# A recurrent layer's output products one unit later, its transposes, scores and second split later

## The chip, the cores and the metric

The kernel runs on one core of a Trainium2 chip. The metric is the device time of one execution in microseconds (us), here the median of three runs. The core has five engines that work from queues of their own: TensorE (PE in the rows; its weight loads are PEld), VectorE (DVE), ScalarE (ACT), GpSimd (POOL) and SyncE (SP), which only issues loads here. DMA transfers are issued by SP and by GpSimd.

## What is computed

Two layers of width 2048 on 256 positions. Layer 0 is a gated mixture with pooling, layer 1 the recurrent layer that the change touches; each is followed by a normalisation, a convolutional feed-forward block and another normalisation. The recurrent layer, cut to what matters:

```python
h = x @ od_w_in[o]                               # 2048 -> 4 x 2048
q, f_logit, inp, g = jnp.split(h, 4, axis=-1)
f = lb + (1.0 - lb) * sigmoid(f_logit)           # 16 heads of 128, chunks of 64 positions
qh, kh, vh = heads(silu(q)), heads(1.0 - f), heads(inp)
bcum = cumsum(heads(log(f)), axis=3)
q_dec, k_dec = qh * exp(bcum), kh * exp(-bcum)
att = where(mask, q_dec @ k_dec.T, 0.0)          # scores
o = att @ vh + q_dec @ state                     # state: decayed sum of k_end.T @ vh
y = rms_norm(o, od_norm_g) * sigmoid(g)          # outputs
mix = y @ od_w_out[o]                            # "down" products
```

## The kernel before

Every product is computed in three parts (high times high, high times low, low times high half of a float32 number), so each weight block of 512 x 512 is loaded from memory as 1 MB and copied twice: ScalarE rounds it to `wh` (line 178), VectorE writes the rest `wl` (line 181). Blocks are used in one fixed list of "feeds". `take` (line 192) hands out the next one, after it has issued the copies of the block two places ahead; three pairs of copies fit. Plain blocks (tag "w") have three raw buffers, loaded by SP as soon as the copy that frees a buffer has been issued and has run.

In the recurrent layer the 16 heads are worked in four head groups `hg`. A head group has two *units*: u0 gives the gates f and g, u1 gives q and the input v. A unit (`strassen`, line 399) multiplies two 1024-row parts by seven products P1 to P7 instead of eight, and the other 1024 rows plainly, as four blocks "s". A product P is 12 matmuls (128 x 128 by 128 x 512), a block "s" 24. P3, P5, P6 and P7 use combinations of the activations (`sh` in the rows), P1, P2, P4 and "s" the activations themselves (`xh`). The weights of P7, P6, P4 come from one raw buffer `a` (tag "qa"), those of P3 and P5 from `b` ("qb"). `a` is loaded by SP when P4 of the unit before has been copied; then GpSimd adds another block onto it by an accumulating load (line 110), which waits until the first load has landed; this sum is P7's operand. After P7's copy another block is accumulated (P6's operand), after P6's copy `b` becomes a - b on VectorE (line 113, P5's operand) and a third block is accumulated onto `a` (P4's operand).

Between the products of a unit stand "o" entries: `down` (line 577), the product of the finished output of an earlier head group with one of four column blocks of `od_w_out`, 2 x 12 matmuls, each half followed by a sum into the residual on VectorE (lines 572 and 574). How many downs a unit has chooses its order from `UNIT_R` (0, 1 or 2 downs). Before the change u0 of group hg has two downs of group hg - 1 and u1 the other two; in group 3 each unit has one, and two follow the units.

The small steps of a head group (gates `pb`, `pe`, `pk`; queries `pq`; scores `pa`, `px`; state `pu`; outputs `po`; transposes of the output `pt`) are put in by due times: `later(n, fn)` (line 314) asks for a step, `tick` (line 317) counts down, and 24 matmuls count as 1. So the order of issue is written by hand through the unit's order and these numbers; the build may still put an instruction ahead of one that it takes not to be ready. Each engine then runs its queue in that order.

Of the kernel before, what the change touches and what calls it, by code (L numbers as in the profile page):

```python
# [10 lines left out]
F32R = mybir.dt.float32r  # L11
# [7 lines left out]
P = 128  # L19
# [8 lines left out]
UNIT_R = (("P1", "P7", "s", "P3", "s", "P6", "P2", "P5", "s", "P4", "s"),  # L28
          ("P1", "s", "P7", "s", "P3", "P2", "P6", "o", "P5", "s", "P4", "s"),
          ("P1", "s", "P7", "s", "P3", "P2", "P6", "o", "P5", "o", "P4", "s", "s"))  # L30
UNIT = ("P1", "s", "P2", "s", "P3", "o", "P7", "o", "P6", "o", "P5", "o", "P4", "s", "s")
BUFS = 3
EDGE = 244
# [2 lines left out]
class Weights:  # L36
# [61 lines left out]
                if ap is not None:  # L98
                    self.std([ap])

    def chain(self, aps, rest, others=()):


        nc = self.nc
        a, b = self._load(aps[3], "qa"), self._load(aps[2], "qb")
        unit = UNIT_R[len(others)]
        rest, others = iter(rest), iter(others)

        def add(ap):
            nc.gpsimd.dma_start(a["tile"].rearrange("p k n -> p (k n)"), ap, accum_op=ALU.add)  # L110

        def t1():
            nc.vector.tensor_tensor(out=b["tile"], in0=a["tile"], in1=b["tile"], op=ALU.subtract)
            add(aps[1])

        a["then"] = lambda: add(aps[2])
        products = {"P7": (a, (), None, lambda: add(aps[0])), "P3": (b,), "P6": (a, (b,), None, t1),
                    "P5": (b,), "P4": (a,)}
        plain = {"P1": aps[0], "P2": aps[1]}
        for f in unit:  # L120
            if f in products:
                self._feed(*products[f])
            else:
                ap = plain[f] if f in plain else next(rest if f == "s" else others, None)
                if ap is not None:
                    self.std([ap])
# [76 lines left out]
def block_kernel(ctx: ExitStack, tc: tile.TileContext, a, out):  # L203
# [42 lines left out]
    W.phase += 1  # L246
    wi, wo = a["w_od_in"], a["w_od_out"]
    for hg in range(4):
        n_out = 2 if hg < 3 else 1
        for u, (c1, c2) in enumerate(((4 + hg, 12 + hg), (hg, 8 + hg))):  # L250
            if hg == 0 and u == 0:
                W.std([wi[c, g] for c in (c1, c2) for g in range(4)])
            else:
                outs = [wo[c, hg - 1] for c in range(u * n_out, (u + 1) * n_out)] if hg else []
                W.chain([wi[c1, 0], wi[c1, 1], wi[c2, 1], wi[c2, 0]],
                        [wi[c1, 2], wi[c1, 3], wi[c2, 2], wi[c2, 3]], outs)
    W.std([wo[c, 2] for c in (2, 3)])
    W.std([wo[c, 3] for c in range(4)])
    plan_ffn(1)
# [15 lines left out]
    def split(dst, src, hs, scale=None):  # L275

        h, l = dst[0][hs], dst[1][hs]
        if scale is None:
            A.activation(h, src, AF.Copy)
            V.tensor_tensor(out=l, in0=src, in1=h.bitcast(F32), op=ALU.subtract)  # L280
        else:
            A.activation(h, src, AF.Copy, scale=scale)
            V.scalar_tensor_tensor(out=l, in0=src, scalar=scale, in1=h.bitcast(F32),
                                   op0=ALU.mult, op1=ALU.subtract)
# [29 lines left out]
    def later(n, fn):  # L314
        waiting.append([n, fn])
# [513 lines left out]
    with ExitStack() as pools:  # L829
# [31 lines left out]
        def heads4(hg):  # L861
# [13 lines left out]
            def after_f(t, ps, f):  # L875
                kh = wk.tile([P, 512], F32, name="kh", tag="tb", bufs=2)
                A.activation(f, ps, AF.Sigmoid)
                V.tensor_tensor(out=f, in0=f, in1=rows["omlb"], op=ALU.mult)
                V.tensor_tensor(out=f, in0=f, in1=rows["lb"], op=ALU.add)
                if t == 1:  # L880
                    rows["ng"] = row("ng", a["norm_g"][qs].rearrange("(o n) -> o n", o=1))
                V.tensor_scalar(out=kh, in0=f, scalar1=-1.0, scalar2=1.0, op0=ALU.mult, op1=ALU.add)
                A.activation(f, f, AF.Ln)
                fh = wk.tile([P, 512], F32R, name="fh", tag="fh", bufs=1)
                fl = wk.tile([P, 512], F32R, name="fl", tag="fl", bufs=1)
                split((fh, fl), f, np.s_[:, :])
                later(1.5 + t, lambda: gates(t, fh, fl, kh))

            def gates(t, fh, fl, kh):

# [30 lines left out]
            def queries(t, q):  # L921
                pq = aux.tile([P, 4, P], F32, name="pq", tag="aux")
                for k in range(4):
                    transpose(pq[:, k], q[:, heads[k]])
                if t == 1:
                    dec = small.tile([P, 4, 1], F32, name="dec")
                    V.tensor_copy(dec, eb[1][:, :, 63:64])
                qd[t] = eb[t]
                V.tensor_tensor(out=qd[t], in0=pq, in1=eb[t], op=ALU.mult)
                if t == 1:  # L930

                    qx[1] = wk.tile([P, 4, P], F32, name="qx", tag="fh", bufs=1)
                    V.tensor_copy(qx[1][:, :, lo], qd[1][:, :, lo])
                    for k in range(4):
                        V.tensor_scalar(out=qx[1][:, k, hi], in0=qd[1][:, k, hi], scalar1=dec[:, k],
                                        scalar2=None, op0=ALU.mult)
                later(1, lambda: scores(t))

            def scores(t):

# [29 lines left out]
            def outputs(t):  # L970
                po = aux.tile([P, 512], F32, name="po", tag="aux")
                mms = [(po[:, hs], att[t][:, k], vv[t][:, hs]) for k, hs in enumerate(heads)]
                if t == 1:
                    mms += [(po[:, hs], qx[1][:, k], st[0][:, k]) for k, hs in enumerate(heads)]
                bank(mms)
                o = wk.tile([P, 512], F32, name="o", tag="tb", bufs=2)
                A.activation(o, po, AF.Copy)
                sq = wk.tile([P, 4, P], F32, name="sq", tag="vv", bufs=2)
                A.activation(sq, o.rearrange("p (k n) -> p k n", k=4), AF.Square)
                ss = small.tile([P, 4], F32, name="ss")  # L980
                V.tensor_reduce(ss, sq, axis=AX.X, op=ALU.add)
                rsqrt(ss, ss, 4, scale=1.0 / P)
                for k, hs in enumerate(heads):
                    V.scalar_tensor_tensor(out=o[:, hs], in0=o[:, hs], scalar=ss[:, k:k + 1], in1=rows["ng"][:, hs],
                                           op0=ALU.mult, op1=ALU.mult)
                V.tensor_tensor(out=o, in0=o, in1=gg[t], op=ALU.mult)
                if t == 0:
                    if hg < 3:
                        y = [yp.tile([P, 4, S], F32R, name=f"y{i}", tag=f"y{i}") for i in "hl"]
                    else:  # L990

                        y = raw[1].tile([P, 2, 4, S], F32R, name="y3", tag="qa")
                        y = [y[:, i] for i in range(2)]
                    YT.append(tuple(y))
                if t == 1 and hg < 3:
                    bounds(hg + 1)
                later(1.5 if hg < 3 else 0.5, lambda: transpose_split(YT[hg], o, t))

            def after_g(t, ps, g):
                A.activation(g, ps, AF.Sigmoid)  # L1000
                gg[t] = g

            def unit(tile1, tile2, done1, done2, downs):
                def tile_of(name, tag):
                    if tag:
                        return wk.tile([P, 512], F32, name=name, tag=tag, bufs=1)
                    return (tile1 if name in ("p1", "u3") else tile2)(name)

                def done(c, tiles):
                    for t in range(2):  # L1010
                        (done1, done2)[c](t, tiles[t])

                strassen(XT, XS[0], tile_of, done, downs, UNIT_R[len(downs)])

            n_out = 2 if hg < 3 else 1
            downs = [lambda c=c: down(c, YT[hg - 1], hg == 1) for c in range(4)] if hg else []
            if hg == 0:
                chunk(XT, 4, lambda t, ps: after_f(t, ps, tile_f()), head=True)
                W.open += 1
                tmp = [wk.tile([P, 4, P], F32, name="cmb", tag=g, bufs=2) for g in ("eb", "eb", "kd", "kd")]  # L1020
                XS.append(combine(XT, *tmp))
                chunk(XT, 4, lambda t, ps: after_g(t, ps, tile_g()))
            else:
                unit(tile_f, tile_g, lambda t, v: after_f(t, v, v), lambda t, v: after_g(t, v, v), downs[:n_out])
            unit(tile_f, tile_i, after_q, after_i, downs[n_out:2 * n_out])
            return downs[2 * n_out:]

        XS = []
        for hg in range(4):
# [83 lines left out]
```

## Time and profile before

| | us |
|---|---|
| median of three runs | 2203.44 (2202.3 to 2204.14) |
| profiled execution | 2202.97 |
| its span, first to last instruction | 2201.2 |
| TensorE busy | 2157.1 (98%) |
| VectorE busy | 1767.4 (80%) |
| ScalarE busy | 1230.3 (56%) |

The recurrent layer lies between about 970 and 1465 us of the span. In a timeline row the number in brackets is the time for which the engine had been idle before the instruction, and behind the arrow what ended that idle time. A row of an accumulating load gives the time at which GpSimd issues it, not when it lands. Matmuls are pipelined: a row's duration is longer than the distance to the next start.

### The profile page before, as it was taken

What the parts mean: (1) busy time and instruction counts of PE and PEld (TensorE: products, weight loads), DVE (VectorE), ACT (ScalarE), POOL (GpSimd) and SP (SyncE); (2) the same over time, 40 slices, a digit from 0 to 9 for tenths busy, and PEclk for the clock granted to TensorE, in tenths of its full rate; (3) what the DMA queues carried; (4) which work ended last, traced back from release to release, by engine and by line L of the source; (5) the groups of instructions that cost most, each with busy time, mean ns of one, the idle gap of its engine ahead of it and who ended that gap; (6) DMA issues with size and microseconds to landing.
All of it is one profiled execution on the core that took longest, in us unless ns stands there. A gap on an engine that the chain in (4) does not pass through costs nothing. (4 is left out here: it accounts for less than half of the span.)

```text
span 2201.2 us, 24814 instructions
## 1 busy us (share of the span) xinstructions
PE 2157.1 (98%) x9887; PEld 1779.9 (81%) x9887; DVE 1767.4 (80%) x1706; ACT 1230.3 (56%) x1150; POOL 125.8 (6%) x140
## 2 busy tenths in 40 slices
PE   9999999999999999989999999999999999999997
PEld 7888788888888888878778888778888888888886
DVE  5545888888888888897687887888888888888888
ACT  5443455555655555646575756636555655555662
POOL 1000200000000000020000000030000000000000
PEclk9999999999999999999999999999999999999999
DMA  8646476777667677537778687746777666677743
GB/s 324 268 151 234 152 243 222 236 247 239 215 217 226 219 241 248 184 128 259 222 236 252 220 256 229 232 173 204 234 243 238 218 223 213 227 241 240 242 150 141
DMA packets 71796, 489.00 MB, mean 222 GB/s; under 512 B 8465, under 2 KB 9121, under 8 KB 13953
## 3 DMA queue, kind: packets, MB, share of 16 engines
q1 hardware_dynamic: 60656, 411.56, 50.0%
q0 software_dynamic: 11024, 75.86, 17.1%
q8 instruction: 77, 1.26, 0.2%
q14 instruction: 39, 0.31, 0.0%
HBM read 443.34 MB, written 2.11 MB: 202 GB/s over the span
## 5 line engine op out<-in xcount | busy, mean ns | idle before, releaser
L181 DVE TENSOR_TENSOR wl<-w,wh 128x2048 fp32r<-128x2048 f32 (+1 forms) x471 | 1051.2, 2235 | 337.7 <-ACT wh L178 334.2
L178 ACT ACTIVATE wh<-w 128x2048 fp32r<-128x2048 f32 (+1 forms) x495 | 894.7, 1813 | 628.7 <-PE pd L566 262.2
L412 PE MATMUL ps<-wh,xh 128*128 128x512 f32 x1188 | 468.0, 394 | 0.0
L412 PE MATMUL ps<-wl,xh 128*128 128x512 f32 x1188 | 462.8, 390 | 1.1 <-DVE wl L181 1.1
L412 PE MATMUL ps<-wh,xl 128*128 128x512 f32 x1188 | 462.8, 390 | 0.0
L566 PE MATMUL pd<-wh,yh 128*128 128x512 f32 x736 | 287.2, 390 | 3.2 <-DVE x L574 3.2
L566 PE MATMUL pd<-wl,yh 128*128 128x512 f32 x736 | 286.5, 389 | 0.4 <-DVE wl L181 0.4
L566 PE MATMUL pd<-wh,yl 128*128 128x512 f32 x736 | 286.4, 390 | 0.5 <-DVE yl L280 0.4
L412 PEld LDWEIGHTS ps<-wh,xl 128*128 128x128 f32 x1188 | 223.0, 188 | 46.7
L412 PEld LDWEIGHTS ps<-wl,xh 128*128 128x128 f32 x1188 | 223.3, 188 | 46.2 <-DVE wl L181 1.9
L412 PEld LDWEIGHTS ps<-wh,xh 128*128 128x128 f32 x1188 | 223.1, 188 | 45.0 <-ACT wh L178 0.4
L412 PE MATMUL ps<-wh,sh 128*128 128x512 f32 x432 | 169.8, 393 | 0.8 <-ACT u L424 0.5
L412 PE MATMUL ps<-wl,sh 128*128 128x512 f32 x432 | 168.9, 391 | 1.1 <-DVE wl L181 1.1
L412 PE MATMUL ps<-wh,sl 128*128 128x512 f32 x432 | 168.7, 390 | 0.0
L566 PEld LDWEIGHTS pd<-wh,yh 128*128 128x128 f32 x736 | 138.2, 188 | 32.5 <-DVE x L574 4.0
L566 PEld LDWEIGHTS pd<-wh,yl 128*128 128x128 f32 x736 | 138.1, 188 | 30.3 <-DVE yl L280 1.6
L566 PEld LDWEIGHTS pd<-wl,yh 128*128 128x128 f32 x736 | 138.2, 188 | 29.3 <-DVE wl L181 0.8
L341 PE MATMUL ps<-wh,xh 128*128 128x512 f32 x384 | 151.8, 397 | 1.6 <-ACT wh L178 1.6
L341 PE MATMUL ps<-wl,xh 128*128 128x512 f32 x384 | 151.2, 394 | 0.3 <-DVE wl L181 0.3
L341 PE MATMUL ps<-wh,xl 128*128 128x512 f32 x384 | 150.8, 393 | 0.0
L789 DVE SCALAR_TENSOR_TENSOR hc<-ph,cw,hc 128x254 f32<-128x254 f32 (+1 forms) x352 | 145.8, 475 | 1.4 <-ACT hc L786 1.2
L786 ACT ACTIVATE hc<-ph,cw 128x256 f32<-128x256 f32 x176 | 89.1, 556 | 62.5 <-DVE hc L789 58.8
(223 smaller groups left out, 2216.5 us busy)
## 6 DMA issues: line engine op xcount, KB each, us to landing
w<-in_w_up SPq DMA_DIRECT2D x176, 1024.0 KB, 4.9
w<-in_w_down SPq DMA_DIRECT2D x88, 1024.0 KB, 4.9
w<-in_w_od_in SPq DMA_DIRECT2D x64, 1024.0 KB, 6.6
w<-w POOLq DMA_DIRECT2D x40, 1024.0 KB, 8.1
w<-in_w_od_in POOLq DMA_DIRECT2D x21, 1024.0 KB, 9.2
w<-in_w_ev_in SPq DMA_DIRECT2D x20, 1024.0 KB, 5.2
w<-in_w_ev_out SPq DMA_DIRECT2D x16, 1024.0 KB, 4.8
w<-in_w_od_out SPq DMA_DIRECT2D x16, 1024.0 KB, 7.2
```

The source lines that it names most:

```text
L178: self.nc.scalar.activation(h[:, sl], w[:, sl], AF.Copy)
L181: eng.tensor_tensor(out=l[:, sl], in0=w[:, sl], in1=h[:, sl].bitcast(F32), op=ALU.subtract)
L341: T.matmul(ps[t], s[:, k, ts], m[:, k], start=(gi == 0 and k == 0 and i == 0), stop=(gi == n - 1 and k == 3 and i == 2))
L412: T.matmul(bank_, x[:, k, ts], m[:, k], start=(id(bank_) not in started), stop=(k == 3 and i == 2), skip_group_check=True)
L566: T.matmul(ps, x[:, k, t * P:(t + 1) * P], m[:, k], start=(k == 0 and i == 0), stop=(k == 3 and i == 2))
L786: A.activation(ob, pt[:, k], AF.Identity, scale=cw[:, 2, blk:blk + 1], bias=cw[:, 3, blk:blk + 1])
L789: V.scalar_tensor_tensor(out=ob[:, s:S], in0=pt[:, k, 0:S - s], scalar=cw[:, w, blk:blk + 1], in1=ob[:, s:S], op0=ALU.mult, op1=ALU.add)
```

## The change

The order of the units is altered: the downs of column blocks 2 and 3 of head group hg - 1 move from u0 and u1 of group hg to u0 of group hg + 1, and blocks 0 and 1 to u1 of group hg. u0 of head group 1 has no down and uses the order for none; u0 of groups 2 and 3 uses a new order, `UNIT_E`, with its two downs right after P1 and P7; u1 of group 3 has two downs. Scores come 1.5 rather than 1 after the queries, output transposes 2 rather than 1.5 after the outputs (groups 0 to 2). The split of the logarithms into two halves is, for the second tile, issued 1.5 later instead of at once, and its gates 1.5 after that, 3 in all rather than 2.5.

```diff
+UNIT_E = ("P1", "o", "P7", "o", "s", "P3", "s", "P6", "P2", "P5", "s", "P4", "s")
...
-        unit = UNIT_R[len(others)]
+        unit = unit or UNIT_R[len(others)]
...
-                outs = [wo[c, hg - 1] for c in range(u * n_out, (u + 1) * n_out)] if hg else []
+
+                outs = [wo[c, hg - 2] for c in (2, 3)] if u == 0 and hg > 1 else []
+                outs += [wo[c, hg - 1] for c in (0, 1)] if u == 1 and hg else []
...
-                        [wi[c1, 2], wi[c1, 3], wi[c2, 2], wi[c2, 3]], outs)
+                        [wi[c1, 2], wi[c1, 3], wi[c2, 2], wi[c2, 3]], outs, UNIT_E if outs and u == 0 else None)
...
-                fh = wk.tile([P, 512], F32R, name="fh", tag="fh", bufs=1)
-                fl = wk.tile([P, 512], F32R, name="fl", tag="fl", bufs=1)
-                split((fh, fl), f, np.s_[:, :])
-                later(1.5 + t, lambda: gates(t, fh, fl, kh))
+
+                def log_split():
+                    fh = wk.tile([P, 512], F32R, name="fh", tag="fh", bufs=1)
+                    fl = wk.tile([P, 512], F32R, name="fl", tag="fl", bufs=1)
+                    split((fh, fl), f, np.s_[:, :])
+                    later(1.5, lambda: gates(t, fh, fl, kh))
+
+                if t == 0:
+                    log_split()
+                else:
+                    later(1.5, log_split)
...
-                later(1, lambda: scores(t))
+                later(1.5, lambda: scores(t))
...
-                later(1.5 if hg < 3 else 0.5, lambda: transpose_split(YT[hg], o, t))
+                later(2 if hg < 3 else 0.5, lambda: transpose_split(YT[hg], o, t))
...
-                unit(tile_f, tile_g, lambda t, v: after_f(t, v, v), lambda t, v: after_g(t, v, v), downs[:n_out])
-            unit(tile_f, tile_i, after_q, after_i, downs[n_out:2 * n_out])
-            return downs[2 * n_out:]
+                unit(tile_f, tile_g, lambda t, v: after_f(t, v, v), lambda t, v: after_g(t, v, v), downs(hg - 2, (2, 3)), UNIT_E if hg > 1 else None)
+            unit(tile_f, tile_i, after_q, after_i, downs(hg - 1, (0, 1)))
+            return downs(hg - 1, (2, 3))
```

## Rows read from the trace of the kernel before

**Rows 1.** The page, part 1: busy us (share of the span) x instructions.
```profile
PE 2157.1 (98%) x9887; PEld 1779.9 (81%) x9887; DVE 1767.4 (80%) x1706; ACT 1230.3 (56%) x1150; POOL 125.8 (6%) x140
```

**Rows 2.** Waits of TensorE, 960 to 1500: us in total, times, longest.
```profile
PE pt L493 <- DVE o L986: 4.2, 3, 1.4
PE pa L943 <- DVE eb L929: 3.3, 1, 3.3
PE ps L412 <- DVE wl L181: 2.2, 3, 1.1
```

**Rows 3.** Timeline, head group 0 to 1: start us, duration us, engine, line, operation.
```profile
1050.06 0.39 PE L412 MATMUL ps<-wh,sh 128*128 128x512 f32 x1
...
1052.78 0.39 PE L412 MATMUL ps<-wh,xh 128*128 128x512 f32 x1
...
1053.43 2.29 DVE L181 TENSOR_TENSOR wl<-w,wh 128x2048 fp32r<-128x2048 f32 x1 [0.57 <-ACT wh L178]
...
1055.75 0.33 SPq L137 DMA_DIRECT2D w<-in_w_od_in  x1
...
1063.53 0.84 POOL L110 DMA_DIRECT2D w<-in_w_od_in  x1 [21.12 <-DVE u L453]
...
1065.53 0.33 SPq L137 DMA_DIRECT2D w<-in_w_od_out  x1
...
1070.84 0.48 PE L412 MATMUL ps<-wh,xh 128*128 128x512 f32 x1
...
1076.75 1.92 ACT L178 ACTIVATE wh<-w 128x2048 fp32r<-128x2048 f32 x1 [9.58 <-DMA w<-in_w_od_in]
...
1078.70 2.29 DVE L181 TENSOR_TENSOR wl<-w,wh 128x2048 fp32r<-128x2048 f32 x1 [10.99 <-ACT wh L178]
```

**Rows 4.** Windows after the two longest waits: busy us (x), PEclk, DMA share, GB/s.
```profile
1081.00:1085.00 4.00, 3.35 (x17) 3.01 (x18) 3.96 (x8) 0.43 (x1) 0.85 (x1) 0.57 0.59 82
1382.00:1385.00 3.00, 3.00 (x8) 2.32 (x8) 2.34 (x3) 3.00 (x2) 0.00 (x0) 0.50 0.97 194
```

**Rows 5.** Timeline, head group 3 between its units.
```profile
1350.81 0.39 PE L412 MATMUL ps<-wh,sh 128*128 128x512 f32 x1
...
1353.01 2.29 DVE L181 TENSOR_TENSOR wl<-w,wh 128x2048 fp32r<-128x2048 f32 x1 [0.32 <-ACT wh L178]
...
1362.86 0.85 POOL L110 DMA_DIRECT2D w<-in_w_od_in  x1 [19.67 <-DMA w<-in_w_od_in]
...
1369.85 0.22 PE L485 MATMUL pb<-tri_r,fh 128*128 128x128 f32 x1
...
1371.57 0.48 PE L412 MATMUL ps<-wh,xh 128*128 128x512 f32 x1
...
1375.03 1.92 ACT L178 ACTIVATE wh<-w 128x2048 fp32r<-128x2048 f32 x1 [4.12 <-DMA w<-in_w_od_in]
...
1376.98 2.29 DVE L181 TENSOR_TENSOR wl<-w,wh 128x2048 fp32r<-128x2048 f32 x1 [5.93 <-ACT wh L178]
...
1386.14 0.39 PE L412 MATMUL ps<-wh,xh 128*128 128x512 f32 x1
```

**Rows 6.** Timeline, head group 2 between its units.
```profile
1243.95 0.85 POOL L110 DMA_DIRECT2D w<-in_w_od_in  x1 [18.67 <-DMA w<-in_w_od_in]
...
1260.00 1.90 ACT L178 ACTIVATE wh<-w 128x2048 fp32r<-128x2048 f32 x1
```

**Rows 7.** Timeline of TensorE: first transposes, P6 and first down of head group 0.
```profile
1099.66 0.52 PE L493 MATMUL pt<-cst,o 128*128 128x128 f32 x3 [0.99 <-DVE ss L500]
...
1103.22 0.48 PE L412 MATMUL ps<-wh,sh 128*128 128x512 f32 x1
...
1107.47 0.39 PE L566 MATMUL pd<-wh,yh 128*128 128x512 f32 x1
...
1114.72 0.39 PE L412 MATMUL ps<-wh,sh 128*128 128x512 f32 x1
```

**Rows 8.** The page, part 3, SP's queue: packets, MB, share of 16 engines.
```profile
q1 hardware_dynamic: 60656, 411.56, 50.0%
```

**Rows 9.** Timeline of TensorE where P7 of the first unit begins.
```profile
1027.93 0.73 PE L412 MATMUL ps<-wh,xh 128*128 128x512 f32 x2
1028.61 0.51 PE L412 MATMUL ps<-wh,sh 128*128 128x512 f32 x1
```

More of the change, by code (lines that the diff above doesn't have):

```diff
@@ L99, in quad, with chain @@
                     self.std([ap])
-    def chain(self, aps, rest, others=()):
+    def chain(self, aps, rest, others=(), unit=None):
         nc = self.nc
         a, b = self._load(aps[3], "qa"), self._load(aps[2], "qb")
-        unit = UNIT_R[len(others)]
+        unit = unit or UNIT_R[len(others)]
         rest, others = iter(rest), iter(others)
@@ L248, in block_kernel @@
     for hg in range(4):
-        n_out = 2 if hg < 3 else 1
         for u, (c1, c2) in enumerate(((4 + hg, 12 + hg), (hg, 8 + hg))):
@@ L1001, in after_g, with unit @@
                 gg[t] = g
-            def unit(tile1, tile2, done1, done2, downs):
+            def unit(tile1, tile2, done1, done2, downs, order=None):
                 def tile_of(name, tag):
@@ L1011, in done, with downs @@
                         (done1, done2)[c](t, tiles[t])
-                strassen(XT, XS[0], tile_of, done, downs, UNIT_R[len(downs)])
-            n_out = 2 if hg < 3 else 1
-            downs = [lambda c=c: down(c, YT[hg - 1], hg == 1) for c in range(4)] if hg else []
+                strassen(XT, XS[0], tile_of, done, downs, order or UNIT_R[len(downs)])
+            def downs(g, cs):
+                return [lambda c=c: down(c, YT[g], g == 0) for c in cs] if g >= 0 else []
             if hg == 0:
```

## Prediction

> **What bounds the kernel now.** I read the page first: TensorE is busy for 2157.1 of 2201.2 us, 98% [rows 1], so the time changes only where TensorE waits or runs slower, and a microsecond of wait is a microsecond of time. The change adds and removes no matrix product: the feed list holds the same twelve down blocks and the same units, in another order. So the sum is one of waits. Next I read who waits for whom in the stage (960 to 1500 us, [rows 2]); there are few: 4.2 us in three waits of output transposes for the gated output `o` (two between head groups, 1.4 each, the third in the tail), 3.3 us in one wait of the score products for `eb`, 2.2 us in three waits for the second copy `wl` of a weight block. Then I read the timeline at each, to see what stood ahead of the late instruction. The page names `eb`; the cause lies elsewhere.
>
> At the boundary from head group 0 to 1 [rows 3] the second product tile is late because VectorE stands at the copy of P7's weights from 1067.7 on (1078.70 less 10.99), that copy waits for ScalarE's, and ScalarE has waited 9.58 us for a DMA, until 1076.75. This DMA is the end of a chain: P4's second copy ends at 1055.72 (1053.43 + 2.29), only then SP may load the block that it frees (1055.75), GpSimd issues the accumulating load on top of it when it has landed (1063.53), it lands at 1076.75, ScalarE and VectorE copy it (to 1078.70 + 2.29 = 1080.99). From the start of P5 (1050.06) that is 30.9 us. After the wait the granted clock is at the lower of its two levels, 1.2 GHz, for part of 1081 to 1085 (mean 0.57 of full, [rows 4]): 4 x 0.43 = 1.7 us more. This boundary costs 3.3 + 1.7 = 5.0 us today.
>
> The last head group's boundary is the same case [rows 5]. P5 starts at 1350.81, P4's copy ends at 1355.30, the DMA lands at 1375.03 after 4.12 us of waiting by ScalarE, the second copy ends at 1379.27: 28.5 us from P5. From 1371.57 to 1386.14 TensorE has 24 + 12 products of 0.227 us (12 take 1052.78 - 1050.06 = 2.72 us, [rows 3]) and the second tile's gates, at most the first tile's 1.72 us (1369.85 to 1371.57): 9.9 of 14.6 us, so 4.7 us are lost, the low clock of [rows 4] in it. Both units end P5, s, P4, s. The middle boundaries end P5, o, P4, s, s: there the accumulating load is issued at 1243.95 and the copy runs at 1260.00 without any DMA wait [rows 6].
>
> **The change, part by part.** (1) *Down blocks one unit later, unit order E.* The new E and the unit without downs both end P5, s, P4, s. So the change takes the two P5, o, P4, s, s endings of the first-half units away, and all four boundaries between units at issue have the short ending. Each down moves its weight load on SP, its two copies and its sums along, but the operand chain that I followed (SP, GpSimd, ScalarE, VectorE) starts from P4's copy and is as long as before.
>
> First boundary: the next unit now begins P1, P7 rather than P1, s, P7. TensorE would reach P7 where it now starts the s block, 1070.84; the second copy ends at 1080.99, so P7 is 9.9 us late (one product of 0.2 runs on the first copy). Two things shorten this. One load of 1 MB (SP's at 1065.53, [rows 3]) is issued later, because its buffer's copy now stands behind P7's on ScalarE; by the load queue's share such a load is 0.500 x 2201.2 x 1.049 / 411.56 = 2.8 us of all DMA engines [rows 8], so the landing gains 0 to 2.8 us; I take the middle, 1.4. And the build may put products of the s block ahead of P7: at 1027.93 two stand ahead [rows 9], where P7 was written first; up to 12 would be 2.7 us, I take two, 0.5. Stall 8.0 (4.4 to 9.9), plus 1.7 of low clock as measured: 9.7 against 5.0 now, +4.7 us.
>
> The Trainium skill (DMA: Bandwidth & Descriptors, Queues, rings and completion order) says that a DMA engine takes turns between the rings that have work. By that rule the accumulating load has its turns however many loads SP has queued, the missing load would gain next to nothing, and the sum below would be 2211.4. The trace's two landings agree (13.2 us with 1063.53 as issue, 12.2 with 1362.86) without telling the rings apart.
>
> Boundaries inside head groups 1 and 2: from P5 to P7 TensorE now has P5, s, P4, s, P1, s = 9 x 2.72 = 24.5 us and the first tile's gates, 1.7: 26.2. The second copy comes at 28.5 [rows 5] to 30.9 [rows 3]: 2.1 to 4.5 us late, new, where today nothing waits. I take 3.3, and 0.9 for the clock (0 to 1.7): 4.2 each, +8.4. In head group 3 the same 4.2 takes the place of 4.7: -0.5.
>
> (2) *The first down of head group 0 and its transposes.* Today the first transpose waits 0.99 us, P6 takes 4.25 us (1103.22 to 1107.47) rather than 2.72 and the down 7.25 (to 1114.72) rather than 5.44, for copies queued on VectorE behind the outputs' sums [rows 7]: 0.99 + 1.53 + 1.81 = 4.3 us. With the downs a unit off and transposes half a step later these go: -4.3 (at least -2.5, should VectorE's queue be late for P5 instead).
>
> (3) *Transposes 2 rather than 1.5 steps, scores 1.5 rather than 1.* A step is 24 products, 5.4 us; the transposes run 2.7 us later relative to their outputs, more than the 1.4 us that they wait. Two of three waits go: -2.8. What hides the later scores is the product stream; GpSimd's power step and the row load behind each output stay behind the same accumulating loads, which are done by then. New on VectorE at the head of E: four sums of downs between two output chains; price 0 to 2 us, bounded by the P6 and down rows of [rows 7]; I take 0, as copies are two blocks ahead. The tail of head group 3 now has P4, s, s and two downs, the outputs half a step further from the end but with half a step less between them: -1.5 to +1, taken as 0.
>
> (4) *The split of the second tile's logarithms.* It leaves ScalarE's queue ahead of the P7 copy and runs 1.5 steps later, its gates at 3 rather than 2.5. In head group 3 its late product was part of the 4.7 counted above. But the second unit's subtraction `b = a - b` is issued on VectorE ahead of P2's copy and waits for an accumulating load that is issued after P7's second copy. P7's copy comes later than now relative to TensorE, so the wait at P2, inside the 2.2 us of [rows 2], should grow and come in three units: 0 to 3, I take +1.5.
>
> **Sum.** +4.7 + 8.4 - 0.5 - 4.3 - 2.8 + 1.5 = +7.0 us on the profiled execution's 2202.97 us: 2210.0. (That run is 0.5 below the median of the three, 2203.44, and its span is 1.8 below its time.) The likeliest case's own range, from its bounds taken partly together, is 2203 to 2217.
>
> **Rivals.** *The short ending is not late in the E units.* If the chain from P5 takes under 26.2 us there, as the unwaited copy of [rows 6] would allow, three boundaries cost nothing: +4.7 - 4.7 - 4.3 - 2.8 = -7.1, 2195.9, faster. For it: E's downs sit at the head, away from the operand chain. Against: SP's loads around the chain are the same, and both short endings seen were late. *P7 is not issued as written.* If the build fills the first boundary with a whole s block, as today's order does, that boundary stays at 5.0 and the sum is +2.3: 2205.3, no change by measurement. *All in time:* if the landing follows the thinner traffic at every boundary, -5.0 - 4.7 - 4.3 - 2.8 = -16.8: 2186.2. *DMA-bound:* two units without downs stand in a row; all terms at their upper bounds give +15 or more: 2218 and up.
>
> **How the numbers follow.** Forecast 0.52 (of it 0.10 within 0.2%), late only at the first boundary 0.17, issued otherwise 0.15, all in time 0.05, DMA-bound 0.11. A measurement of this kernel tells about 0.2%, 4.4 us, from no change. Faster 0.22, same 0.25, slower 0.53. The range 2194 to 2218 leaves out the two outer cases, 0.16.
>
> **What would show it.** In the changed profile: ScalarE's first copy of P7 waiting on a DMA at four boundaries, TensorE idle before the first `sh` product after P1 of head group 1 for about 8 us; no waits of transposes between head groups; the first down at 5.4 us. If ScalarE shows no DMA waits of over 2 us at the middle boundaries, the second term is wrong; if TensorE goes from P1 into s there, the first.

## The result and the profile after

The changed kernel takes 2223.7 us (median of five runs, 2216.52 to 2230.24) against 2204.14 (2202.3 to 2208.05) for the kernel before: a ratio of 1.009, 95% interval 1.0069 to 1.0111, so it is slower by 15 to 24 us. The sign was predicted; the 2210.0 was too low, and the range ended at 2218. The profiled execution took 2227.97 us, 4.3 above that median; its span is 2226.3. Page of the changed kernel, part 1 (columns as in [rows 1]):

```profile
PE 2160.3 (97%) x9887; PEld 1783.2 (80%) x9887; DVE 1768.2 (79%) x1706; ACT 1229.6 (55%) x1149; POOL 128.5 (6%) x140
```

The same 9887 products; the 25.1 us between the two spans are waits and slow products. Waits of TensorE in the stage, 960 to 1530 us (columns as in [rows 2]):

```profile
PE pb L487 <- ACT fh L281: 26.0, 3, 11.4
...
PE ps L414 <- ACT p L426: 5.9, 2, 5.7
PE pt L495 <- DVE o L995: 3.7, 4, 1.2
PE ps L414 <- DVE wl L182: 0.2, 1, 0.2
```

A new line leads: 26.0 us in three waits for `fh`, the high half of the logarithm that the change postponed. Where they lie, in the timeline of TensorE; the first row is the boundary of [rows 3], the others are those inside head groups 1, 2 and 3:

```profile
1077.85 0.80 PE L414 MATMUL ps<-wh,sh 128*128 128x512 f32 x1 [5.69 <-ACT p L426]
...
1082.94 0.39 PE L414 MATMUL ps<-wh,xh 128*128 128x512 f32 x1
...
1141.91 0.48 PE L487 MATMUL pb<-tri_r,fh 128*128 128x128 f32 x1 [5.56 <-ACT fh L281]
...
1272.80 0.47 PE L487 MATMUL pb<-tri_r,fh 128*128 128x128 f32 x1 [11.42 <-ACT fh L281]
...
1273.37 0.78 PE L414 MATMUL ps<-wh,sh 128*128 128x512 f32 x1
...
1278.01 0.22 PE L487 MATMUL pb<-tri_r,fl 128*128 128x128 f32 x1
...
1400.78 0.48 PE L487 MATMUL pb<-tri_r,fh 128*128 128x128 f32 x1 [9.02 <-ACT fh L281]
```

After each wait the twelve products of P7 run slower than the 2.72 us of [rows 3]: 5.09 at the first (1077.85 to 1082.94), 4.64 in head group 2 (1273.37 to 1278.01), 5.18 and 5.27 in 1 and 3; the granted clock from 1077 to 1083 is 0.53 on the mean, so partly at 1.2 GHz, after TensorE had stood still. So the four boundaries cost 5.69 + 2.37 = 8.1, 5.56 + 2.46 = 8.0, 11.42 + 1.92 = 13.3 and 9.02 + 2.55 = 11.6 us: 41.0 where the kernel before lost 5.0 + 4.7.

The line names `fh`, as [rows 2] named `eb`; again the cause is further up. Timeline of ScalarE in the changed kernel (start, duration, engine, line, operation; in brackets the idle time before it):

```profile
1073.12 1.91 ACT L179 ACTIVATE wh<-w 128x2048 fp32r<-128x2048 f32 x1 [8.01 <-DMA w<-in_w_od_in]
...
1077.21 0.59 ACT L426 ACTIVATE p<-ps 128x512 f32<-128x512 f32 x1
...
1131.84 1.92 ACT L179 ACTIVATE wh<-w 128x2048 fp32r<-128x2048 f32 x1 [4.45 <-DMA w<-in_w_od_in]
...
1262.74 1.91 ACT L179 ACTIVATE wh<-w 128x2048 fp32r<-128x2048 f32 x1 [10.29 <-DMA w<-in_w_od_in]
1264.67 1.28 ACT L885 ACT_TABLE_LOAD   x1
1265.96 0.63 ACT L885 ACTIVATE u<-u 128x512 f32<-128x512 f32 x1
1266.61 1.28 ACT L1009 ACT_TABLE_LOAD   x1
1267.91 0.63 ACT L1009 ACTIVATE c<-c 128x512 f32<-128x512 f32 x1
1268.54 1.28 ACT L907 ACT_TABLE_LOAD   x1
1269.83 0.60 ACT L907 ACTIVATE eb<-pb 128x512 f32<-128x512 f32 x1
...
1271.59 0.63 ACT L916 ACTIVATE ke<-pe 128x512 f32<-128x512 f32 x1
1272.07 0.68 ACT L281 ACTIVATE fh<-u 128x512 fp32r<-128x512 f32 x1
1272.59 0.64 ACT L426 ACTIVATE p<-ps 128x512 f32<-128x512 f32 x1
...
1390.72 1.91 ACT L179 ACTIVATE wh<-w 128x2048 fp32r<-128x2048 f32 x1 [7.92 <-DMA w<-in_w_od_in]
```

Four times ScalarE stands idle at the copy of P7's weights until the accumulating load lands, as forecast. What was not: behind the copy, in the same queue, stand the logarithm of the second tile (L885), the sigmoid of the second gate tile (L1009), the exponentials (L907 to L916), `fh`, and the emptying of P1's bank (L426), which P7 needs. With three loads of the function table they take from 1264.67 to 1273.23, beginning only when the load has landed. TensorE resumes with P7 at 1273.37, 10.6 us after the landing; in head groups 1 and 3 it is 10.6 as well (1131.84 to 1142.48, 1390.72 to 1401.35). The kernel before has another order in the same queue; ScalarE, head group 3, the rows around the copy at 1375.03 of [rows 5]:

```profile
1368.34 0.63 ACT L1000 ACTIVATE c<-c 128x512 f32<-128x512 f32 x1
...
1370.28 0.63 ACT L883 ACTIVATE u<-u 128x512 f32<-128x512 f32 x1
...
1376.85 0.61 ACT L279 ACTIVATE fh<-u 128x512 fp32r<-128x512 f32 x1
```

There the sigmoid and the logarithm were done while the load was on its way, and `fh` came 1.82 us after the landing. In head group 2 the first tile's exponentials stood ahead of the copy too.

The Trainium skill (ScalarE: Activation LUTs, What ACT_TABLE_LOAD costs) puts a switch of tables at 1.28 us for the load and 1.38 for a drain, 2.66 in all. The load agrees (1.28); no drain shows: the copy ends at 1264.65, the logarithm starts at 1265.96, 1.31 us later. By the page's sum the three switches would take 8.0 us rather than 3.9.

### The profile page after: what moved, and what is told of

Its sections match the earlier page's. It is cut to its first block, busy times and chain, and to the rows that moved or that the text cites. A ratio compares the mean times of both kernels' runs of the same rounds, so it can differ in the third digit from the quotient of the medians.

```text
span 2226.3 us, 24800 instructions
## 1 busy us (share of the span) xinstructions
PE 2160.3 (97%) x9887; PEld 1783.2 (80%) x9887; DVE 1768.2 (79%) x1706; ACT 1229.6 (55%) x1149; POOL 128.5 (6%) x140
```

## The experiments

Ratios are to the kernel before, run on the same chip between the runs, with 95% intervals. Two theories stood at first: L, the load chain of P7's operand with ScalarE's queue behind it; S, the postponed split. Others (rival M: the later scores and transposes) are named with the runs.

**Which part of the change.** `split_back` is the changed kernel with the split at once and its gates at 1.5 + t again; `split_alone` is the kernel before with the postponed split and nothing else; `downs_alone` is the kernel before with only the downs moved and order E.

```diff
 # split_back, in the changed kernel
-                if t == 0:
-                    log_split()
-                else:
-                    later(1.5, log_split)
+                log_split()
```

> The changed kernel with the second tile's split of logarithms put back (issued at once, its gates 2.5 after). Theory L (the load chain of the unit's ending is late, and ScalarE works off a queue of about 8 us behind the late copy of P7 before TensorE can go on): the copy of P7 is as late as in the changed kernel, the half fh comes a few places earlier, P1's evacuation no earlier; the waits at the three boundaries inside head groups 1 to 3 move to another instruction and stay within 3 us each: 2215 to 2228 us. Rival S (the postponed split is the cause: TensorE waits for fh in all three): the three waits of 26 us in sum and the low clock after them go, 2190 to 2207 us.

> The kernel before with the second tile's split of logarithms postponed, nothing else. Theory L: no wait appears in head groups 1 and 2, whose units have the long ending and where the copy of P7 is in time; in head group 3, with a late copy now and then, the boundary stays within 5 us of its 4.7: 2200 to 2209 us. Rival S: waits for fh of 5 us or more at all three boundaries, 2218 us or more.

> The kernel before with the down blocks one unit later and order E alone: scores, transposes and the split of logarithms at their old due times. Theory L: the loss is the unit endings', so it is all here: fh waits of 10 us or more at the middle boundaries, transposes waiting 1.4 us each again, 2217 to 2230 us. Rival M (the later scores and transposes make the loss, by moving output work into the window where the late load stands): 2196 to 2208 us.

Measured: `split_back` 2223.09 us, 1.009 (1.0072 to 1.0107); `split_alone` 2201.96, 1.0001 (0.9986 to 1.0016); `downs_alone` 2219.18, 1.008 (1.0052 to 1.0108). So the split costs nothing that can be told, alone or in the change, although the longest waits carry its name; moved downs and E carry nearly all of the loss. S and M fall. Two finer signs of L failed in `downs_alone`: its `fh` waits in the middle are 0.35, 5.34 and 5.19 us, not 10 (other waits of the same steps follow them), and between head groups no transpose waits for `o`, though its due times are those of the kernel before. In `split_back`, with the later due times, two wait 0.82 us each.

**Is it the load, and what stands behind it?** `no_first_add` leaves out the first accumulating load of each unit (P7's operand lacks one of its two blocks). `no_gate_sigmoid` leaves out the sigmoid of gate g in head groups 1 to 3. `long_ending` only changes E.

```diff
 # no_first_add
-        a["then"] = lambda: add(aps[2])
 # no_gate_sigmoid
-                A.activation(g, ps, AF.Sigmoid)
+                if ps is not g:
+                    A.activation(g, ps, AF.Sigmoid)
 # long_ending
-UNIT_E = ("P1", "o", "P7", "o", "s", "P3", "s", "P6", "P2", "P5", "s", "P4", "s")
+UNIT_E = ("P1", "o", "P7", "o", "P3", "s", "P6", "P2", "s", "P5", "P4", "s", "s")
```

> The changed kernel without the first accumulating load of each unit of the recurrent layer: P7 uses the first block alone, a part of the computation left out. The order of issue stays. Theory L: P7's operand lands some 12 us earlier, no ScalarE wait for it over 2 us, all four boundaries run without a wait: the changed kernel less 8, 8, 13 and 11 us, 2182 to 2192 us. Rival S: fh is issued at the same place, the three waits for it stay by more than half: 2205 us or more.

> The changed kernel with one part of the computation left out: the sigmoid of gate g in head groups 1 to 3 (the raw gate goes into the output instead). At three boundaries this takes one reload of the function table (1.28 us) and one sigmoid of a 128x512 tile (about 0.6 us) off ScalarE's queue, between the late copy of P7's weights and the split fh that TensorE waits for. Theory L (TensorE waits for the load and then for what is queued behind it on ScalarE): TensorE resumes 8.7 rather than 10.6 us after the landing, the fh waits fall from 26.0 to about 20 us, 2213 to 2220 us for the changed kernel's 2223.7. Rival D (the lateness of the load alone sets the end, ScalarE's queue is hidden behind VectorE's copy): fh waits or whatever takes their place stay, 2221 to 2226 us.

> The changed kernel with one line other: UNIT_E ends P2, s, P5, P4, s, s rather than P2, P5, s, P4, s, downs still after P1 and P7. From P4's copy to P7 TensorE then has as much work as in the middle units of the kernel before. Theory L: ScalarE's wait for the DMA and TensorE's wait for fh go in head groups 2 and 3 (11.4 and 9.0 us and some 2 us of low clock behind each), the one in head group 1 stays: 2198 to 2208 us. Rival S: the split stands as in the changed kernel, the waits stay: 2215 us or more. Rival B (too much DMA traffic): the same bytes in the same time, the waits stay within a few us.

Measured: `no_first_add` 2188.27 us, 0.9933 (0.9919 to 0.9948); `no_gate_sigmoid` 2211.63, 1.0052 (1.0035 to 1.0069); `long_ending` 2206.68, 1.0014 (1.0001 to 1.0028). All three within what L expected, or 1.4 us better. Waits of TensorE in `no_first_add`:

```profile
PE pb L486 <- ACT fh L280: 3.1, 3, 1.0
```

Without the load 26.0 us of `fh` waits are 3.1. In `no_gate_sigmoid` more went than the sigmoid and its table: the build then also put the emptying of P1's bank ahead of the exponentials, and TensorE resumed 4.4 us after the landing, where 8.7 was expected. ScalarE and TensorE there, head group 2:

```profile
1256.95 1.92 ACT L179 ACTIVATE wh<-w 128x2048 fp32r<-128x2048 f32 x1 [7.73 <-DMA w<-in_w_od_in]
...
1260.72 0.58 ACT L426 ACTIVATE p<-ps 128x512 f32<-128x512 f32 x1
```

```profile
1261.35 0.80 PE L414 MATMUL ps<-wh,sh 128*128 128x512 f32 x1 [2.75 <-ACT p L426]
```

`long_ending` has no `fh` wait in head groups 2 and 3, but keeps one after the unit whose ending is still short (4.15 us in head group 1) and 9.69 us at the first boundary.

**Is it the ending?** That would follow from the prediction's step, so the kernel before was given the short ending.

```diff
-           ("P1", "s", "P7", "s", "P3", "P2", "P6", "o", "P5", "o", "P4", "s", "s"))
+           ("P1", "s", "P7", "s", "P3", "P2", "P6", "o", "o", "P5", "s", "P4", "s"))
```

> The kernel before with one edit: the order for two downs ends o, o, P5, s, P4, s rather than o, P5, o, P4, s, s (P4 is one block nearer to the unit's end, nothing else changes place by more than a block). Theory L (it is the distance from P4 to the next P7 that decides): at the boundaries inside head groups 1 and 2, where the kernel before waits for nothing, ScalarE waits for the accumulating load and TensorE for what follows it, 6 to 10 us each: 2213 to 2223 us. Rival C (it is the number of downs in a unit that decides, the whole length of the unit against the whole chain of its operand): 2198 to 2207 us.

Measured: 2201.08 us, 0.9997 (0.9981 to 1.0014). The ending alone costs nothing in the units of the kernel before: theory L in this form is refuted, and with it the prediction's step from the ending to a late load. In the units of order E the ending does matter, as `long_ending` shows. ScalarE of `short_ending_before`, head group 2:

```profile
1257.76 0.62 ACT L1000 ACTIVATE c<-c 128x512 f32<-128x512 f32 x1
...
1259.69 0.63 ACT L883 ACTIVATE u<-u 128x512 f32<-128x512 f32 x1
1260.23 1.90 ACT L178 ACTIVATE wh<-w 128x2048 fp32r<-128x2048 f32 x1
1262.04 0.61 ACT L279 ACTIVATE fh<-u 128x512 fp32r<-128x512 f32 x1
```

Two things differ from the changed kernel. The load is there by 1260.23, at most 20.0 us after the start of P5 (1240.22), where the changed kernel needs 27.8 (1234.90 to 1262.74). And the logarithm and the sigmoid stand ahead of the copy. GpSimd's issue, which comes when the load of `a` has landed, splits the first difference; the changed kernel, and `short_ending_before`:

```profile
1249.03 0.84 POOL L111 DMA_DIRECT2D w<-in_w_od_in  x1 [21.16 <-DMA w<-in_w_od_in]
```

```profile
1250.11 0.85 POOL L110 DMA_DIRECT2D w<-in_w_od_in  x1 [23.89 <-DMA w<-in_w_od_in]
```

SP issues the load of `a` 5.3 and 4.5 us after P5's start (1240.21 and 1244.70); it takes 8.8 and 5.4 us, and the accumulating load 13.7 and at most 10.1. So at least 7.0 us of the difference lie in the two transfers. Windows of this stretch (DMA share is the last column but one); the changed kernel, `short_ending_before`, and the kernel before while it loads `a`:

```profile
1240.00:1249.00 9.00, 9.00 (x42) 7.44 (x41) 7.80 (x9) 6.33 (x6) 0.00 (x0) 1.00 0.94 327
1249.00:1256.00 7.00, 7.00 (x39) 5.95 (x38) 4.91 (x6) 3.42 (x5) 1.42 (x2) 1.00 1.00 246
```

```profile
1244.00:1250.00 6.00, 6.00 (x29) 4.95 (x28) 3.56 (x3) 2.96 (x2) 0.00 (x0) 1.00 0.68 206
1250.00:1255.00 5.00, 5.00 (x24) 4.14 (x23) 4.47 (x3) 4.17 (x4) 0.85 (x1) 1.00 1.04 295
```

```profile
1237.50:1244.00 6.50, 6.50 (x31) 5.37 (x30) 5.69 (x7) 4.40 (x5) 0.05 (x1) 1.00 0.90 309
```

E puts its two downs at the head and runs P6, P2, P5 in a row. SP issued the two loads ahead of that of `a` 6.3 and 3.1 us before it there, in `short_ending_before` 9.6 and 5.1. While `a` is loaded the engines are at 0.94 rather than 0.68. The share alone is no measure of lateness: the kernel before has 0.90 there, its load of `a` takes 6.4 us (1237.54 to 1243.95), and nothing waits.

**Is it the traffic?** Theory T says so. `thin_loads` halves every plain weight load of the units with P7 in the changed kernel and uses the half twice; `thin_ending` does so for the third and fourth s block alone; `more_traffic` adds 1 MB per unit to the kernel before.

```diff
 # thin_loads: where r["part"] is 2
-            self.nc.sync.dma_start(w[:, k:k + n].rearrange("p k n -> p (k n)"),
-                                   r["ap"][:, k * 512:(k + n) * 512])
+            self.nc.sync.dma_start(w[:, k:k + m].rearrange("p k n -> p (k n)"),
+                                   r["ap"][:, k * 512:(k + m) * 512])
 # more_traffic, ahead of the load of tag "qa"
+            self.nc.sync.dma_start(x[:, 0:2048], r["ap"][:, 0:2048])
```

> The changed kernel with part of the computation left out: in the units with P7 every plain weight block (P1, P2, s, down) is loaded by half (0.5 of 1 MB) and the half is used twice; copies, products, order and the accumulating loads are as they were. A unit then moves 4 to 5 MB less, some 11 to 14 us of all DMA engines at 2.8 us for 1 MB. Theory T (the operand of P7 lands late because the unit's other loads keep the DMA engines busy): the fh waits and the wait at the first boundary all but go, 2186 to 2196 us. Rival C (the steps from P6's copy to the next P7, subtract, accumulate, copy, load, accumulate, are too long by themselves for the 29.7 us that this order gives them): the fh waits stay at 8 us or more, 2212 to 2224 us.

> As thin_loads, but only the third and fourth s block of each such unit, those after P5 and P4, are loaded by half (the other half left out and the first used twice): 1 MB less in each unit's ending, 2.8 us of all DMA engines. Theory T: P7's operand lands 2.8 to 5 us earlier at each of four boundaries, 2206 to 2215 us. Rival C: 2218 to 2226 us, as the changed kernel.

> The kernel before with one more transfer in each unit with P7: 1 MB copied within the device's memory, issued by SyncE just ahead of the load that follows P4's copy. Nothing waits for it. Theory T: where the kernel before waits for nothing (the boundaries inside head groups 1 and 2) or for 4 to 5 us, P7's operand lands 2.8 to 6 us later, with what follows on ScalarE; 2209 to 2224 us. Rival C (transfers are not what is short): 2199 to 2207 us.

Measured: `thin_loads` 2209.3 us, 1.0041 (1.0024 to 1.0058); `thin_ending` 2220.49, 1.0102 (1.0069 to 1.0136); `more_traffic` 2202.01, 1.0011 (0.9993 to 1.0028). T is half right at best: all plain loads halved give back some 11 us, a quarter of that traffic nothing that can be told, and more traffic does not hurt the kernel before by anything that can be told. Rival C gave the right times for the last two, but falls with the first: with the distances unchanged the load lands earlier there and the time is below C's 2212. ScalarE of `thin_loads`, head group 2:

```profile
1246.77 1.92 ACT L190 ACTIVATE wh<-w 128x2048 fp32r<-128x2048 f32 x1 [1.51 <-DMA w<-in_w_od_in]
...
1256.11 0.68 ACT L292 ACTIVATE fh<-u 128x512 fp32r<-128x512 f32 x1
```

The load lands 19.1 us after P5 (1227.70) and not 27.8, ScalarE waits 1.51 us for it, and still `fh` comes 9.3 us later, behind the same queue. In head groups 1 and 3 the load gains less, 21.2 against 23.3 us and 22.8 against 25.5. Three `fh` waits of 12.5 us in all remain. This left the place in the queue.

**Is it the place in ScalarE's queue?** Theory Q. `copy_behind_gates` is the changed kernel with an order given to the build: the copy of P7's weights comes after the second tile's logarithm and sigmoid. `copy_behind_thin` has the halved loads too.

```diff
             c = self.nc.scalar.activation(h[:, sl], w[:, sl], AF.Copy)
+            while self.behind:
+                self.tc.add_manual_dep(c.ins, self.behind.pop().ins.name,
+                                       mybir.DependencyInfo(mybir.DependencyClass.NoSync, mybir.DependencyReason.DATA),
+                                       reason="behind the gates")
...
+                i = A.activation(f, f, AF.Ln)
...
+                i = A.activation(g, ps, AF.Sigmoid)
+                if hg and t == 1:
+                    W.behind += [i, *ln1]
```

> The changed kernel with one thing more: in head groups 1 to 3 ScalarE's copy of P7's weights is put behind the logarithm of the second tile of f and the sigmoid of the second tile of g in ScalarE's queue, as the kernel before has it in head groups 2 and 3; nothing else changes, but the two sigmoids now stand together and one reload of the function table (1.28 us) goes. Theory Q (TensorE loses what stands in ScalarE's queue behind the late copy; in the changed kernel the copy stands ahead of these steps, which wait idle behind it): TensorE resumes 6 to 6.5 us after the landing rather than 10.6, 4 us less at each of three boundaries, 2207 to 2213 us. Rival T (the landing alone sets it, some other step takes the place): fh or p waits as large as before, 2218 to 2226 us.

> copy_behind_gates and thin_loads together (plain weight blocks of the units with P7 loaded by half and used twice, part of the computation left out). If the landing and the queue behind it are the two parts of the loss, the three waits for fh, 12.5 us in thin_loads, all but go: 2192 to 2200 us. If thin_loads' rest has another cause: 2203 to 2210 us, as thin_loads.

Measured: 2208.84 us, 1.0025 (1.0006 to 1.0044), and 2194.65, 0.9971 (0.9955 to 0.9988), both as Q expected. (In head group 2 the kernel before has only the logarithm ahead of the copy; its second sigmoid runs at 1261.80, behind it.) ScalarE and TensorE of `copy_behind_gates`, head group 2:

```profile
1246.43 0.63 ACT L1018 ACTIVATE c<-c 128x512 f32<-128x512 f32 x1
1247.08 1.28 ACT L890 ACT_TABLE_LOAD   x1
1248.38 0.63 ACT L890 ACTIVATE u<-u 128x512 f32<-128x512 f32 x1
1253.88 1.92 ACT L179 ACTIVATE wh<-w 128x2048 fp32r<-128x2048 f32 x1 [4.87 <-DMA w<-in_w_od_in]
...
1259.34 0.67 ACT L286 ACTIVATE fh<-u 128x512 fp32r<-128x512 f32 x1
```

```profile
1260.55 0.79 PE L419 MATMUL ps<-wh,sh 128*128 128x512 f32 x1 [5.23 <-ACT p L431]
```

The load lands 25.0 us after P5 (1228.85), still late, but TensorE resumes 6.7 us after it, not 10.6. The four kernels make a square, in ratios to the kernel before: changed 1.009, queue mended 1.0025, loads thinned 1.0041, both 0.9971. The queue is worth 0.65 points, 14 us, the traffic 0.49, 11 us, both 1.19, 26 us: they add up, each to within some 0.3 points by the intervals. The part of the traffic is the less certain: with the same halved loads the operand lands 24.4 us after P5 in head group 2 of `copy_behind_thin` (1222.69 to 1247.04), where `thin_loads` has 19.1. What is left, 0.29% faster than the kernel before (6 us), is of the size that the change was found to save elsewhere (6.0 us, next section); its profile still shows 7.7 us of waits at the four boundaries, where the kernel before lost 9.7.

**Other orders.** `long_endings_2` gives u1 of head group 1 one block more ahead of P7, `long_endings_3` also changes the unit without downs, and the last two spread the downs again, one into u0 of head group 1. In `long_endings_3` the third s block comes ahead of P5 and shares a PSUM bank with it, so part of that block is added into P5's result: a part of the computation is changed, not the instructions.

> The changed kernel with order E ending P5, P4, s, s, as in long_ending, and beside it the u1 units of head group 1 alone in a new order, P1, s, o, P7, s, P3, P6, P2, o, P5, P4, s, s, with P7 one block later and P5 and P4 next to each other. Theory L: the fh wait that was left in head group 1 (4.15 us) goes, since P7 comes 5.4 us later after P1, the first boundary's 9.7 stays: 2196 to 2204 us. Rival (the wait left there is of ScalarE's queue, not of the load): 2205 to 2209 us.

> As long_endings_2, and u0 of head group 1 (the unit without downs) begins P1, s, P7 rather than P1, P7, and has P5 and P4 further from its end: P1, s, P7, s, P3, P6, P2, s, P5, P4, s. Theory L: at the first boundary a block of 5.4 us lies ahead of P7, its wait falls from 9.7 to about 4, as in the kernel before: 2189 to 2199 us, below the kernel before by 4 to 13 us. Rival (the load is as late relative to P7, since it starts from P4's copy which moves too, or the operand of the next unit becomes late instead): no better than long_endings_2, 2196 to 2206 us.

> The changed kernel with its downs spread otherwise: 1 in u0 of head group 1, 2 in each unit up to u0 of head group 3, 1 in its u1, 2 after the units as in the kernel before; E is P1, o, P7, s, P3, s, P6, P2, o, P5, P4, s, s, and u0 of head group 1 runs P1, s, P7, s, P3, P6, P2, o, P5, P4, s, s; scores in head group 3 at 1 as before. Theory L: every boundary between units that waits in either kernel then has the long ending or one block more ahead of P7, 1 to 3 us stay at the first: 2190 to 2199 us. Rival (the unit with one down is shorter than its operand's chain, so what the boundary gains is lost at P6 and P4): 2199 to 2207 us.

> As spread_downs, with P1, s, o, P7, s, P3, P6, P2, o, P5, P4, s, s for the u0 of head groups 2 and 3 and the u1 of head group 1: one block more from P4 to the next P7, one block less from P7 to P6. Theory L with the measured waits of long_endings_2 (5 us of wl waits in the one unit of that order): 2196 to 2206 us, slower than spread_downs by 3 to 8 us. Rival (only the boundary counts): the same as spread_downs within 2 us.

Measured: 2206.88 us, 1.0027 (1.0014 to 1.004); 2202.48, 1.0002 (0.9987 to 1.0018); 2200.44, 1.0004 (0.9989 to 1.0019); 2203.38, 1.0011 (0.9994 to 1.0029). The first three missed what L expected, by 1.4 to 3.5 us, and lie in the ranges of their rivals; the fourth is in L's range, but its 2.9 us to `spread_downs` are within the intervals. In `long_endings_2` the `fh` wait went, but waits for the second copy `wl` grew from 4.7 to 10.3 us: one block taken from the stretch from P7 to P6. `spread_downs` has no wait for `fh` and none over 0.2 us at P7 left and is still no faster than the kernel before: its unit with one down waits 1.3 and 2.5 us at its later copies. None of the kernels that leave the computation whole beats the kernel before.

## Why the prediction was wrong

**First boundary, +4.7: right in kind, too large.** ScalarE waited for the DMA and TensorE stood after P1 without running the s block, as said. The cost is 8.1 - 5.0 = +3.1. Counted from P5 the load landed after 22.0 us (1051.13 to 1073.12) where the kernel before had 26.7, 4.7 sooner; I had allowed 1.4. It landed 10.7 us after its issue (1062.44), against 13.2 in [rows 3], which speaks against the round robin of the Trainium skill (DMA: Bandwidth & Descriptors, Queues, rings and completion order) as I had applied it; but `long_ending`, with the same order there, took 13.2 again (1063.17 to 1076.37), so the runs don't decide it.

**Boundaries inside head groups, +8.4 and -0.5: the step that failed.** Measured 8.0 and 13.3, and 11.6 - 4.7 = +6.9: 28.2 where I had 7.9. The landing was sized well, 23.3 to 27.8 us after P5 where my rows gave 24.2 (1350.81 to 1375.03) to 26.7 (1050.06 to 1076.75). What failed is its end: I let the stall end with VectorE's second copy, 4.2 us after the landing, since [rows 5] ended so. In the changed kernel ScalarE's queue holds 8.6 us of work behind the copy, and TensorE resumes 10.6 us after the landing: 6.4 us more at each of three boundaries, 19 of the 20.3 us by which these two terms were short. I read the late copy's own row in [rows 5] and not the rows around it, which would have shown that the neighbours happened to stand ahead. The reason that I gave for the late landing, the ending P5, s, P4, s, is not enough besides: `short_ending_before` has it and loses nothing. So the good size of the landing is in part luck.

**First down and its transposes, -4.3: right.** In the changed kernel these transposes wait for nothing, P6 takes 3.37 us (1108.54 to 1111.91) and the first down 5.44 (1162.25 to 1167.69) from start to the next start: -3.7. **Transposes between groups, -2.8: too large, and for the wrong reason.** Two waits of 0.82 remain of 1.42 each: -1.2. `downs_alone` has none of them at the old due times, so in these runs the moved downs took the waits away and the later due time brought part of them back. **P2's wait, +1.5: wrong in sign.** The `wl` line fell from 2.2 to 0.2, but 1.14 of the 2.2 was the wait at P6 that the -4.3 already holds; at P2 it was 0.64 and 0.43, and none is left: -1.1. That a queue which stands still at P7 gives the later copies time is a guess. These three save 6.0 us.

**Sum.** 3.1 + 28.2 - 6.0 = +25.3. Of the 25.1 us between the profiled spans 1.1 were there before the first boundary (P5 of the first unit starts at 1051.13 rather than 1050.06), so 24.0 were to be explained; -1.3 stay unassigned. **Rivals.** *DMA-bound* had the time (2218 and up) but not the reason: traffic is 11 of some 26 us, and by itself did nothing to the kernel before. *The short ending is not late in the E units* was wrong of E, though short endings without E are in time in `short_ending_before`. *P7 is not issued as written* fell: TensorE stood after P1. *All in time* was worked out as 2186.2; with the accumulating load left out (`no_first_add`) it is 2188.27, with the queue mended and the loads thinned 2194.65. **What stays open:** why the build places the copy ahead of the gates in the changed kernel. The source order there is the same in both kernels; that it takes the load to be ready sooner is a guess, which no run shows. And which of E's transfers make the operand land later was not separated.

## What to carry to other kernels

Price a late transfer not by its own consumer but by everything that stands behind that consumer in its engine's queue and has been ready all along: read the rows of that engine on both sides of the copy, in the kernel that will run. When a change moves work, the order in the queues can change where the source does not, so look at whether a copy that may wait stands ahead of short steps on the critical path, and put it behind them by an explicit order. The name on the longest wait (`fh`) is not the cause: undoing the edit that carries the name gave back nothing.

## What the runs showed of the hardware

The packets of the accumulating load take the DMA engines about twice as long as those of a plain one. Part 3 of the page, GpSimd's queue (packets, MB, share of 16 engines), of the changed kernel and of `no_first_add`:

```profile
q0 software_dynamic: 11024, 75.86, 17.0%
```

```profile
q0 software_dynamic: 10016, 68.52, 15.5%
```

0.170 x 2226.3 - 0.155 x 2188.1 = 39 us for 7.34 MB, 5.4 us a megabyte, against 2.7 for SP's queue [rows 8]. The changed kernel's five runs lie 13.7 us apart, the four of `no_first_add`, without the load that is waited for, 2.2. That the wait makes the spread isn't shown: the four runs of `split_back`, which waits for the load as well, lie 4.2 apart.
